# Last norm of a mixture-of-experts stage split into three steps, GpSimd's order written out, and two experts that finish their tokens in place

## The chip, the cores and the metric

The kernel runs on one core of a Trainium2 chip (trn2). The metric is the device time of one execution in microseconds (us), lower is better; three runs of the kernel before gave 2713.91, 2713.98 and 2725.86 us, median 2713.98 us.

## The reference, cut to what matters

2048 tokens of width 1024, all in float32, pass a first block, a second mixer with its norm, cross attention with its norm, and last a grouped mixture of experts (MoE) with a residual and a layer norm. Only that last part is touched.

```python
def grouped_moe(x, router_w, router_bias, w_gate, w_up, w_down):
    scores = sigmoid(xt @ router_w)                       # 16 experts in 4 groups of 4
    sel = scores + router_bias
    best = argmax(sum of the top 2 of sel in each group)  # one group for each token
    _, idx = top_k(where(in_grp, sel, -inf), 2)           # two experts, both of that group
    gate = scores[idx] / sum(scores[idx])
    # for each expert, blocks of 128 of its tokens:
    hb = silu(xb @ w_gate[e]) * (xb @ w_up[e])            # 1024 -> 256
    yb = hb @ w_down[e]                                   # 256 -> 1024
    return sum over the two experts of gate * yb

x = layer_norm(DEEPNORM_ALPHA * x + grouped_moe(x, ...), ln_moe_g, ln_moe_b)
```

## The kernel before, in words

Matrix products are done in float32 by splitting each operand in a rounded high part (a cast on ScalarE, line 173) and a low part (a subtraction on VectorE or GpSimd, line 174), and three matmuls (`mm3`). Weights come by DMA from SyncE's queue (`rawload`), six loads of 512 KB for an expert, into a ring of seven buffers, and are split as they come.

The MoE stage, `moe()`, starts at about 2222 us of the span and lasts to its end. By then a DRAM table `x3d` holds each token's row and its gates, and a DRAM table `sumd` holds the scaled residual, to which the experts' results are added. The router has put, for each expert, the numbers of its tokens into a table `tabi`. `BLOCKS` says how many blocks of 128 tokens an expert has a place for: two or three. The first two are one **unit** (`n` = 2, matmuls over 256 tokens), a third is a unit of its own (`n` = 1) that uses the same weights: 23 units in all, in the order of the experts 0 to 15. Tokens beyond that would be worked off in a loop at the end (`For_i` over `nit`); for these inputs it runs no pass.

`run` emits the units as a pipeline. In the iteration of a unit `u` (its neighbours are `v`, the next, and `w`, the one after):

1. `u.up(0)`: half of gate and up, 48 matmuls (24 for a third block); splits of down weights; `u.act(0)`: tanh on ScalarE, two steps on VectorE (lines 1175, 1176), a cast and a subtraction.
2. `turn` of the unit before (two transposes, third blocks alone), then the hook `mids`.
3. `u.up(1)`, `u.act(1)`; the transposes of `v`'s gathered tokens (line 240) with their splits; the last gate-and-up weights of `v`; the indirect gather of `w`'s tokens on GpSimd's queue (line 1126).
4. `down` of the unit before: 12 matmuls for a block, scaled on ScalarE out of PSUM (line 1200), and an indirect scatter-add into `sumd` on GpSimd's queue (line 1201). Each scatter-add waits until those of the unit before and the fetches since have landed, since rows may be the same.
5. The hook `late`, then the splits of `w`'s weights.

The last norm needs a token's finished sum. A token's two experts are of one group, so a group's tokens are done when its four experts are. For them a second table `tabgi` lists the tokens of each group in blocks of 128 (`NFIN` blocks: 4, 5, 5, 4, and 2 for the tokens of expert 15, which comes last). `last_norm`, called by the hooks as `FETCH` says (one or two blocks for an expert from expert 5 on), fetches one block of sums (`fetch`, line 1395) and at the same place finishes the block fetched one expert earlier (`finish`): statistics on VectorE (line 1410), one over the standard deviation by two small GpSimd instructions (lines 192 and 194, result `fr`), two passes over 128x1024 on VectorE (line 1417 with the mean, line 1418 with `fr`), and an indirect write to the output on GpSimd's queue (line 1419). At the end stand the blocks of the last groups, first with statistics alternating between VectorE and ScalarE (lines 1405, 1406).

What sets the order: ScalarE and VectorE run in the order in which the program is written (`MANUAL`). The orders of TensorE and GpSimd come from the tile scheduler, which places each instruction where its own estimate of time puts it. Each engine runs its list in order, so an instruction that waits holds all behind it on its engine; GpSimd is also the engine that issues all indirect DMAs.

## Time and profile before

| | us |
|---|---|
| median of three runs | 2713.98 |
| the profiled execution: its time | 2722.46 |
| the profiled execution: span, first to last instruction | 2720.7 |
| of the span: up to the MoE stage | 2222 |
| MoE stage: 2222 to the last matmul | 458 |
| after the last matmul, to the end of the span | 40 |

An execution's time is 1.8 us more than its span (2722.46 less 2720.7). The profiled execution is 8.5 us longer than the median of the three runs. TensorE is busy for 94% of the whole span; in the MoE stage the granted clock, the waits of TensorE and the stretch after the last matmul are what is to be read, and the section of rows below has them. The profile's chain of waits reaches back only 1.3 us from the end here and says nothing.

### The profile page before, as it was taken

To read this page: it belongs to the slowest core of one execution; us is meant where nothing else is said; L and a number is where in the kernel's file an instruction comes from. 1 tells how busy PE (TensorE), PEld (TensorE's weight loads), DVE (VectorE), ACT (ScalarE), POOL (GpSimd) and SP (SyncE) were. 2 spreads that over 40 slices of the span, in tenths; PEclk is the share of its full clock that TensorE was granted. 3 is DMA by queue.
4 is the path that set the end of the run, shared out by engine and by line. 5 is a ranking of instruction groups with operands and counts; after the bars stand their busy time and mean duration, and the time that the engine had idled before them with its cause. 6 is when DMAs were issued, how large, how long until landed. Compare 5 with 4: busy or idle time off the path is not lost. (4 is left out here: it accounts for less than half of the span.)

```text
span 2720.7 us, 36998 instructions
## 1 busy us (share of the span) xinstructions
PE 2549.0 (94%) x13954; PEld 2156.0 (79%) x13954; DVE 1608.8 (59%) x3228; ACT 1136.1 (42%) x2023; POOL 597.4 (22%) x635
## 2 busy tenths in 40 slices
PE   8899999999999999999999999999999969989882
PEld 8777788777878887778788878778888859978872
DVE  5536366766454666665456666563667457666554
ACT  5644353242444532434354333343532325444442
POOL 0102202211021031101201221021032133445445
PEclk9999999999999999999999999999999979999986
DMA  8861351444224325441242345312415357878755
GB/s 299 287 217 55 109 163 55 154 152 145 92 77 133 117 64 169 155 141 48 84 161 72 116 144 197 94 55 87 162 47 183 104 180 264 247 237 254 223 153 138
DMA packets 121557, 396.81 MB, mean 146 GB/s; under 512 B 15264, under 2 KB 15408, under 8 KB 121376
## 3 DMA queue, kind: packets, MB, share of 16 engines
q1 hardware_dynamic: 104144, 334.01, 36.6%
q0 software_dynamic: 17232, 60.42, 8.4%
q8 instruction: 110, 1.80, 0.3%
q14 instruction: 71, 0.58, 0.1%
HBM read 314.87 MB, written 81.60 MB: 146 GB/s over the span
## 5 line engine op out<-in xcount | busy, mean ns | idle before, releaser
L183 PE MATMUL bank<-rounded 128*128 128x512 f32 (+2 forms) x10628 | 2198.8, 364 | 73.4 <-ACT rounded L173 54.1
L183 PEld LDWEIGHTS bank<-rounded 128*128 128x128 f32 x10628 | 1773.3, 192 | 380.4 <-ACT rounded L173 61.5
L174 DVE TENSOR_TENSOR rounded<-work,rounded 128x1024 fp32r<-128x1024 f32 (+3 forms) x531 | 577.7, 1100 | 476.4 <-ACT rounded L173 430.4
L173 ACT CAST rounded<-work 128x1024 fp32r<-128x1024 f32 (+3 forms) x564 | 512.5, 926 | 691.2 <-PE bank L183 251.8
L173 ACT CAST rounded<-bank 128x512 fp32r<-128x512 f32 (+1 forms) x220 | 112.0, 555 | 219.1 <-PE bank L240 98.1
L183 PE MATMUL bank<-work 128*128 128x128 f32 (+5 forms) x944 | 163.6, 301 | 6.9 <-DVE work L525 2.2
L183 PEld LDWEIGHTS bank<-work 128*128 128x128 f32 (+1 forms) x944 | 130.7, 190 | 37.0 <-issue 5.1
L174 DVE TENSOR_TENSOR rounded<-bank,rounded 128x512 fp32r<-128x512 f32 (+1 forms) x220 | 133.0, 639 | 42.5 <-ACT rounded L173 40.6
L240 PE MATMUL bank<-ident,work 128*128 128x128 f32 x712 | 98.2, 283 | 28.4 <-ACT work L345 8.6
L240 PEld LDWEIGHTS bank<-ident,work 128*128 128x128 f32 x712 | 82.2, 145 | 46.3 <-ACT work L345 13.4
L192 POOL TENSOR_SCALAR lnrv<-lnmv 128x1 f32<-128x1 f32 x32 | 40.6, 1269 | 283.3 <-DVE lnmv L672 283.1
L375 POOL TENSOR_SCALAR work<-work 128x512 f32<-128x512 f32 x32 | 25.4, 793 | 345.9 <-ACT work L374 345.9
L665 DVE SCALAR_TENSOR_TENSOR work<-work,bank 128x512 f32<-128x512 f32 x64 | 43.8, 685 | 73.3 <-PE bank L183 73.1
L1201 POOL DMA_INDIRECT sumd<-work,tabi x39 | 72.1, 1849 | 35.1 <-ACT work L1200 15.7
L174 POOL TENSOR_TENSOR rounded<-work,rounded 128x1024 fp32r<-128x1024 f32 (+1 forms) x33 | 65.9, 1997 | 38.1 <-ACT rounded L173 35.4
L754 DVE SCALAR_TENSOR_TENSOR work<-work,c_convT 128x512 f32<-128x512 f32 x96 | 71.9, 749 | 2.5 <-ACT work L752 0.7
L1126 POOL DMA_INDIRECT work<-x3d,tabi x39 | 47.9, 1228 | 113.9 <-issue 42.1
L859 POOL TENSOR_TENSOR work<-work 128x512 f32<-128x512 f32 (+6 forms) x40 | 46.2, 1154 | 112.3 <-ACT work L851 110.4
L192 POOL TENSOR_SCALAR rrmsv<-ssq 128x1 f32<-128x1 f32 x34 | 11.2, 329 | 261.4 <-DVE ssq L570 172.7
L795 POOL TENSOR_TENSOR work<-work,ar 128x520 f32<-128x520 f32 x16 | 17.0, 1062 | 232.8 <-DVE work L757 177.3
L906 POOL TENSOR_SCALAR work<-work,xrv 128x256 f32<-128x256 f32 x64 | 30.1, 484 | 152.3 <-DVE xrv L904 152.3
L1200 ACT ACTIVATE work<-bank,gr 128x512 f32<-128x512 f32 x78 | 51.1, 702 | 29.4 <-PE bank L183 13.0
(320 smaller groups left out, 2148.1 us busy)
## 6 DMA issues: line engine op xcount, KB each, us to landing
work<-in_w_gu SPq DMA_DIRECT2D x64, 512.0 KB
work<-in_x SPq DMA_DIRECT2D x32, 512.0 KB
work<-in_w_out SPq DMA_DIRECT2D x32, 512.0 KB
work<-wmp SPq DMA_DIRECT2D x32, 512.0 KB
work<-wxa SPq DMA_DIRECT2D x32, 512.0 KB
work<-wvw SPq DMA_DIRECT2D x32, 512.0 KB
work<-in_w_dn SPq DMA_DIRECT2D x32, 512.0 KB
sumd<-work SPq DMA_DIRECT2D x19, 512.0 KB
```

The costliest lines, as they stand in the source:

```text
L173: ACT.copy(hi, src)
L174: (lo_eng or DVE).tensor_sub(lo, src, f32(hi))
L183: PE.matmul(o, l, r, start=start, stop=stop)
L192: POOL.tensor_scalar(v, src, scale, eps, op0=OP.mult, op1=OP.add)
L240: PE.transpose(p[:, k * 128:(k + 1) * 128], src[:, (4 * hf + k) * 128:(4 * hf + k + 1) * 128], ident)
L665: DVE.scalar_tensor_tensor(oh_, xr, ALPHA, a, op0=OP.mult, op1=OP.add)
L754: DVE.scalar_tensor_tensor(s, z[:, k:k + T], conv[:, k, c:c + 1], s, op0=OP.mult, op1=OP.add)
L859: POOL.tensor_tensor(nx[:, lo:], cur[:, lo:], cur[:, lo - d_:15 + T - d_], op=OP.add)
L906: POOL.tensor_scalar(P[:, h, :], P[:, h, :], rv[:, h:h + 1], 0.0, op0=OP.mult, op1=OP.add)
L1126: POOL.indirect_dma_start(out=xg, out_offset=None, in_=x3d[:, :], in_offset=at)
L1200: ACT.activation(y[:, hs], a, AF.Copy, scale=self.gc[r])
L1201: d = POOL.indirect_dma_start(out=sumd[:, :], out_offset=self.at[r], in_=y, in_offset=None, compute_op=OP.add)
```

## The change

- **Order of the experts.** `ORDER` is 0 to 7, 12, 13, 8, 9, 10, 14, 11, 15.
- **Finished in place.** Experts 11 and 15 (`FINAL`) stand at the end of their groups, 2 and 3. Each of their blocks fetches the sums of its tokens ahead (`sums`), VectorE adds the gated result out of PSUM to them (line 1228 in the changed kernel, in the place of ScalarE's scaling), and the block is normed and written from there. The sum is still written to `sumd`, now by a plain scatter in the place of the adding one. Their tokens leave the group tables: `NFIN` is 3, 5, 2, 3, so 13 blocks are fetched for the norm in the place of 20, and 5 more are finished in place.
- **Three steps.** `fetched` (the new hook `turn`, before the gather of `w` and before `down`) fetches one or two blocks; `measure`, in the next iteration's `mids`, takes the statistics and `fr`; `norms`, in that iteration's `late`, does the two passes and the write. The loose constants of `FETCH` are gone: one block is fetched, or two where three or more are ready or a `FINAL` unit comes next.
- **GpSimd's order.** `queued` ties each GpSimd instruction of the stage that it is given to the one before, without a wait, so that the scheduler keeps the written order. The small scalar step (line 193) is left free.
- **Buffers.** The key and value tables of the first block are joined as `sks`, whose first 1024 columns serve as a fourth buffer `FX` of fetched sums.
- **The end.** The last three blocks of group 3 have statistics and the multiplication by `fr` on ScalarE and the addition of the bias on GpSimd (line 1461, `shared`); the blocks of experts 11 and 15 have theirs on VectorE, with statistics on ScalarE for every first one.

```diff
+ORDER = 0, 1, 2, 3, 4, 5, 6, 7, 12, 13, 8, 9, 10, 14, 11, 15
+FINAL = 11, 15
-FETCH = {5: (1, 0), 6: (1, 0), 7: (1, 0), ...}
...
-    NL = 5
-    NFIN = 4, 5, 5, 4, 2
+    NL = 4
+    NFIN = 3, 5, 2, 3
...
+        FX = rotate([FX((128, D)) for _ in range(3)] + [sks[:, 0:D]])
...
+        def queued(*ds_):
+            if line[0]:
+                for d in ds_:
+                    for o in line[1]:
+                        tc.add_manual_dep(d.ins, o.ins.name, mybir.DependencyInfo(
+                            mybir.DependencyClass.NoSync, mybir.DependencyReason.DATA), reason="order")
+            line[1] = ds_
+            return ds_[0]
...
+            def sums(self, mem):
+                self.z = [fetch(at, mem)[0] for at in self.at]
...
-                    y = YT((128, D))
+                    y = self.z[r] if self.final else YT((128, D))
...
-                        ACT.activation(y[:, hs], a, AF.Copy, scale=self.gc[r])
+                        if self.final:
+                            DVE.scalar_tensor_tensor(y[:, hs], a, self.gc[r], y[:, hs], op0=OP.mult, op1=OP.add)
+                        else:
+                            ACT.activation(y[:, hs], a, AF.Copy, scale=self.gc[r])
                     d = POOL.indirect_dma_start(out=sumd[:, :], out_offset=self.at[r], in_=y, in_offset=None,
-                                                compute_op=OP.add)
+                                                compute_op=OP.bypass if self.final else OP.add)
...
+                    if self.final:
+                        queued(d)
+                        measured.append((y, self.at[r], *stats(y, DVE if r else ACT), True, YT))
...
                     v.weights_up([3])
+                    if i in turn:
+                        turn[i]()
                     if w:
                         w.gather()
                     if i:
                         units[i - 1].down()
                     if i in late:
                         late[i]()
...
+        def scaled(z, at, mean, op, r, static=True, mem=None, shared=False):
+            x = mem((128, D)) if mem else z
+            DVE.scalar_tensor_tensor(x, z, mean, gains[:, 0], op0=op, op1=OP.mult)
+            if shared:
+                ACT.activation(x, x, AF.Copy, scale=r)
+                queued(POOL.tensor_tensor(x, x, gains[:, 1], op=OP.add))
+            else:
+                DVE.scalar_tensor_tensor(x, x, r, gains[:, 1], op0=OP.mult, op1=OP.add)
+            d = POOL.indirect_dma_start(out=out[:, :], out_offset=at, in_=x, in_offset=None,
...
+        def fetched(j):
+            if units[j].final:
+                units[j].sums(FX)
+            if j == N - 2:
+                fetches(len(ready), XG)
+            elif not units[j].final:
+                fetches(1 if len(ready) < 3 and not units[j + 1].final else 2)
+
+        for j in range(5, N - 1):
+            mids[j], turn[j], late[j] = measure, lambda j=j: fetched(j), norms
...
         def last():
-            last_norm(30, 1)
-            group_done(3)
-            last_norm(0, NFIN[3], XG)
+            norms()
+            measure(ACT, 1)
+            units[N - 1].sums(MRAW)
+
+        mids[N - 1], late[N - 1] = last, lambda: (measure(ACT), norms())
```

On **GpSimd**, where a block is fetched in the middle of the stage (before: around expert 11; in the rows `x3d` is a gather of tokens, `sumd<-work` a scatter-add, `work<-sumd` a fetch for the norm, `frv` and `fr` the two small instructions, `out_dram` the write), there stands before:

```order
L1126 DMA work<-x3d,tabi 128x1040
L1201 DMA sumd<-work,tabi 2432x1024
L1395 DMA work<-sumd,tab 128x1024
L192 TENSOR_SCALAR frv_17216<-fmv_17208 128x1
L194 TENSOR_TENSOR fr_17220<-frv_17216,mhalf 128x1
L1419 DMA out_dram<-work,tab 2048x1024
L1126 DMA work<-x3d,tabi 128x1040
```

and now, where the third block of expert 12 and the first two of expert 13 are worked on, up to the gathers for expert 8:

```order
L1436 DMA sks<-sumd,tab 128x1024
L1436 DMA work<-sumd,tab 128x1024
L1146 DMA work<-x3d,tabi 128x1040
L1231 DMA sumd<-work,tabi 2432x1024 x2
L193 TENSOR_SCALAR frv_17049<-fmv_17041 128x1
L195 TENSOR_TENSOR fr_17053<-frv_17049,mhalf 128x1
L193 TENSOR_SCALAR frv_17050<-fmv_17042 128x1
L195 TENSOR_TENSOR fr_17054<-frv_17050,mhalf 128x1
L1436 DMA work<-sumd,tab 128x1024 x2
L1146 DMA work<-x3d,tabi 128x1040 x2
L1231 DMA sumd<-work,tabi 2432x1024
```

Before, the fetch of a block stands between the scatter-adds and the `fr` of another block, and one gather of each pair stands ahead of the adds. Now the fetches stand ahead of the gathers and the adds, and `fr` stands ahead of the next fetches; both gathers of a pair stand behind the fetches.

On **VectorE**, in the iteration of a unit of two blocks (before: expert 11; `bank` is PSUM, `L1175` and `L1176` are `act`, `fmv` the statistics), there stands before:

```order
L174 TENSOR_TENSOR rounded<-bank_70,rounded 128x128
L1410 BN_STATS fst_17211<-work 128x6 x2
L1411 BN_AGGR fmv_17208<-fst_17211 128x2
L1417 SCALAR_TENSOR_TENSOR work<-work,fmv_17208 128x1024
L1418 SCALAR_TENSOR_TENSOR work<-work,fr_17220 128x1024
L1175 SCALAR_TENSOR_TENSOR work<-work,bank_71 128x256
L1176 TENSOR_TENSOR work<-work,bank_71 128x256
```

and now (expert 13):

```order
L1451 BN_STATS fst_17045<-sks 128x6 x2
L1452 BN_AGGR fmv_17041<-fst_17045 128x2
L1451 BN_STATS fst_17044<-work 128x6 x2
L1452 BN_AGGR fmv_17042<-fst_17044 128x2
L1198 SCALAR_TENSOR_TENSOR work<-work,bank_67 128x256
L1199 TENSOR_TENSOR work<-work,bank_67 128x256
L175 TENSOR_TENSOR rounded<-work,rounded 128x256
L175 TENSOR_TENSOR rounded<-bank_68,rounded 128x512
L175 TENSOR_TENSOR rounded<-bank_69,rounded 128x512
L1339 COPY gr_15872<-work 128x1
L1458 SCALAR_TENSOR_TENSOR sks<-sks,fmv_17041,work 128x1024
L1463 SCALAR_TENSOR_TENSOR sks<-sks,fr_17053,work 128x1024
```

Only the statistics are left ahead of the second activation (`L1198`, before `L1175`); the pass that needs `fr` has moved behind it and behind the splits of the next unit's tokens.

On **GpSimd**, at the very end, there stands now, from the fetch of expert 15's sums on (`out_dram<-work,tab` are group 3's blocks, `out_dram<-work,tabi` those of expert 15):

```order
L1436 DMA work<-sumd,tabi 128x1024 x2
L193 TENSOR_SCALAR frv_17049<-fmv_17041 128x1
L195 TENSOR_TENSOR fr_17053<-frv_17049,mhalf 128x1
L1461 TENSOR_TENSOR work<-work 128x1024
L1464 DMA out_dram<-work,tab 2048x1024
...
L1464 DMA out_dram<-work,tab 2048x1024
L1231 DMA sumd<-work,tabi 2432x1024
L195 TENSOR_TENSOR fr_17054<-frv_17050,mhalf 128x1
L1231 DMA sumd<-work,tabi 2432x1024
L195 TENSOR_TENSOR fr_17055<-frv_17051,mhalf 128x1
L1464 DMA out_dram<-work,tabi 2048x1024 x2
```

Before, the last matmuls were followed by two scatter-adds, two fetches that wait for them, and the norms of both; now the two scatters stand between the norms, and no fetch is left behind the last matmul.

## Rows read from the trace of the kernel before

**Rows 1.** Head of the page.

```profile
span 2720.7 us, 36998 instructions
```

**Rows 2.** Windows: stretch, length, busy by engine (instructions), PEclk, DMA share, GB/s.

```profile
2240.00:2360.00 120.00, 119.01 (x885) 113.71 (x883) 85.82 (x193) 65.36 (x101) 44.47 (x27) 0.99 0.80 249
2360.00:2660.00 300.00, 261.43 (x1743) 240.93 (x1742) 184.90 (x308) 133.21 (x229) 138.12 (x108) 0.93 0.74 218
2680.00:2721.00 41.00, 0.31 (x2) 0.00 (x0) 17.62 (x18) 7.88 (x14) 22.57 (x23) 0.53 0.42 124
```

**Rows 3.** Waits, 2390 to 2660: who <- for whom: us in total, times, longest.

```profile
POOL work L1395 <- DMA sumd<-work,tabi: 40.8, 7, 9.2
DVE work L1418 <- POOL fr L194: 40.4, 11, 6.9
...
PE bank L183 <- ACT rounded L173: 28.3, 7, 7.2
```

**Rows 4.** TensorE's waits alone, 2390 to 2660.

```profile
PE bank L183 <- POOL rounded L174: 5.9, 2, 3.9
```

**Rows 5.** Timeline, 2511 to 2528: start, us, engine, line [idle before <- releaser].

```profile
2511.54 1.58 POOL L1201 DMA_INDIRECT sumd<-work,tabi  x1 [0.30 <-issue]
...
2522.44 1.00 POOL L1395 DMA_INDIRECT work<-sumd,tab  x1 [9.32 <-issue]
...
2523.78 0.57 POOL L194 TENSOR_TENSOR fr<-frv,mhalf 128x1 f32<-128x1 f32 x1
2524.39 1.28 DVE L1418 SCALAR_TENSOR_TENSOR work<-work,fr 128x1024 f32<-128x1024 f32 x1 [6.06 <-POOL fr L194]
...
2527.43 8.39 PE L183 MATMUL bank<-rounded 128*128 128x256 f32 x48 [4.91 <-ACT rounded L173]
```

**Rows 6.** TensorE's timeline, pieces after waits and pieces without.

```profile
2488.88 8.81 PE L183 MATMUL bank<-rounded 128*128 128x256 f32 x48 [3.99 <-ACT rounded L173]
...
2567.20 1.91 PE L240 MATMUL bank<-ident,work 128*128 128x128 f32 x16
...
2580.31 6.00 PE L183 MATMUL bank<-rounded 128*128 128x256 f32 x48
...
2586.93 3.01 PE L183 MATMUL bank<-rounded 128*128 128x512 f32 x12
...
2628.19 7.59 PE L183 MATMUL bank<-rounded 128*128 128x256 f32 x48 [4.32 <-ACT rounded L173]
...
2642.37 13.43 PE L183 MATMUL bank<-rounded 128*128 128x512 f32 x68 [3.91 <-POOL rounded L174]
...
2675.20 5.11 PE L183 MATMUL bank<-rounded 128*128 128x512 f32 x12 [7.71 <-ACT rounded L173]
```

**Rows 7.** DMA issues, 2230 to 2660: count, median us from issue to landing.

```profile
work<-x3d,tabi POOLq DMA_INDIRECT x39, 8.3
sumd<-work,tabi POOLq DMA_INDIRECT x36, 8.9
work<-sumd,tab POOLq DMA_INDIRECT x13, 4.2
```

**Rows 8.** Instructions that write or read `sumd`, 2340 to 2610: DMA landing.

```profile
DMA to landing us min/median/max: 4.2/8.9/12.0
```

**Rows 9.** GpSimd's groups, 2230 to 2721: count, busy us, mean ns.

```profile
L1201 POOL DMA_INDIRECT sumd<-work,tabi x39 | 72.1, 1849 | 35.1 <-ACT work L1200 15.7 <-issue 9.9 <-DMA work<-sumd,tab 4.5
...
L174 POOL TENSOR_TENSOR rounded<-work,rounded 128x1024 fp32r<-128x1024 f32 x13 | 35.0, 2691 | 2.4 <-ACT rounded L173 2.3
L1419 POOL DMA_INDIRECT out_dram<-work,tab x20 | 22.6, 1129 | 20.3 <-DVE work L1418 14.8 <-DVEq L1471 1.6 <-DMA work<-sumd,tab 1.6
```

**Rows 10.** Timeline after the last matmuls: a pair of ScalarE statistics, and the last instruction.

```profile
2672.38 1.06 ACT L1405 ACTIVATE junk<-work 128x1024 bf16<-128x1024 f32 x1 [7.20 <-DMA work<-sumd,tab]
...
2674.67 0.19 ACT L1406 ACTIVATION_READ_ACCUMULATOR junk<-work,fmv 128x1 f32 x1
...
2711.73 1.03 POOL L1419 DMA_INDIRECT out_dram<-work,tab  x1 [1.61 <-DVEq L1471]
```

107 lines of the change are left out of this document (62 added, 45 removed).

## The prediction, as it was put on record

> **What bounds the kernel now.** I first read the windows by stage. From 2240 to 2360, with no norm yet, TensorE is busy 119.0 of 120 us at full granted clock; from 2360 to 2660, where norms run beside the experts, it is busy 261.4 of 300 at a mean clock of 0.93; from 2680 to the end at 2720.7 it does nothing [rows 1, 2]. So TensorE bounds the stage, and it loses time in two ways: it waits among the norms, and nothing is left for it at the end.
>
> Then the waits, to see for whom it waits. Between 2390 and 2660 it waits seven times, 28.3 us, for a cast of ScalarE (line 173), and twice, 5.9 us, for a weight split on GpSimd [rows 3, 4]. VectorE waits 40.4 us in 11 pieces for `fr`, and GpSimd's fetches wait 40.8 us for scatter-adds to land [rows 3].
>
> Last the timeline, where these are one chain. GpSimd issues a scatter-add at 2511.54; the fetch behind it can only be issued at 2522.44, 10.9 us later; `fr` of another block, which needs neither, stands behind it and is made at 2523.78; VectorE's second pass starts at 2524.39 after 6.06 us of waiting, and only then come the activation steps behind it; TensorE starts again at 2527.43 after 4.91 us [rows 5]. VectorE's pass ends at 2525.67, so the activation and the casts take 1.8 us more. That a norm is late costs nothing by itself; that the activation stands behind it in VectorE's list does.
>
> **The waits that go.** The change takes the pass with `fr` out from in front of the activation, and `fr` out from behind a blocked fetch. The seven waits (28.3) and the two for GpSimd's late split (5.9) are 34.2 us [rows 3, 4]. What hides the passes now is the matmuls of `down` and of the next unit's first half. I take all 34.2 as gone; the bound below is that those for GpSimd stay (28.3), since its list is as full as before.
>
> After such a wait the matmuls are slow, too: 48 of them take 6.00 us where none precedes, and 8.81, 8.39 and 7.59 after waits of 3.99, 4.91 and 4.32 [rows 5, 6], that is 2.8, 2.4 and 1.6 us more, 2.3 on average. This is the granted clock falling from 2.4 GHz to 1.2 for a while. Of the nine waits, six are over 2.9 us; six times 2.3 is 13.8 us. Bounds: nothing, and the 21 us that 0.93 of 300 us leaves, idle time included [rows 2].
>
> **The waits that come.** GpSimd's list is now fixed, and its fetches and scatter-adds wait for one another: a fetch for the landing of the last add, an add for the landing of the fetches. Both gathers of a unit stand behind the fetches. The worst place is where two iterations in a row fetch two blocks each, before expert 8's gathers. From the issue of the add of expert 7's third block: first fetch at 10.9 (as in [rows 5]), second at 12.2 (1.00 and a gap of 0.30), landed 4.2 later at 16.4 [rows 7]; two adds for expert 12, the second 1.85 + 0.30 later at 18.6 [rows 9]; its landing, again 10.9, lets the next fetch go at 29.5, the second at 30.8, the gathers at 32.1 and 33.4; they land 8.3 later, at 40.4 and 41.7 [rows 7]. Beside that TensorE has: the third block of expert 12 with 6.00, transposes for expert 13 with 1.91, expert 12's down with two times 3.01; expert 13's 12.0, its third block's transposes of half 1.91, the down of a third block 3.0, the next 48 matmuls 6.00 [rows 6]: 35.9 us together. The second tile's transposes can wait the 0.95 of the first, so the wait is 41.7 - 0.95 - 35.9 = 4.9 us; with 2.3 for slow matmuls 7.2. The same chain stands once more, from the add of expert 10's third block over experts 14 and 11 to the gathers for expert 15. Two times 7.2 is 14.4 us. Adds landing at their median of 8.9 rather than 10.9 would take 4 us from each chain and leave 0.9; at the largest, 12.0 [rows 8], it is 2.2 more, 7.1.
>
> In front of experts 5 and 6 the statistics of two blocks now stand where VectorE has the group tables to work out; I put 2 us there, between 0 and the 3 us or so that GpSimd's and VectorE's small steps of two blocks take.
>
> Everything else has one answer. The 20 blocks become 18, off the path. The order of experts moves no work of TensorE. The joined table `sks` leaves the first block's instructions in their order. Finishing in place trades ScalarE's scaling for a VectorE addition out of PSUM of the same size. GpSimd gets one more power step for nothing.
>
> **The end.** Before, the first half of expert 15's matmuls ends at 2642.37 + 13.43 = 2655.8 [rows 6] and the span at 2720.7 [rows 1]: 64.9 us, with 7.71 of waiting before the last matmuls [rows 6], two adds that must land, two fetches, and their norms. Counted from the same point, the new end has, in ScalarE's list, the second half (6.0) and expert 11's third block (3.0), 9.0; three pairs of statistics of 2.5 (2672.38 to 2674.86 [rows 10]), 16.5; the activation 1.8 and as an estimate 0.4 for the tanh ahead of it, 18.7; a fourth pair 21.2; a scaling of 1.1 as the 1.06 pass in [rows 10], 22.3. From there GpSimd is the bound: three additions of 128x1024, which I price as its 2.69 us subtraction of the same shape, each with a write of 1.13 and a gap of 0.30 [rows 9]: 12.4, to 34.7; then two scatters of 1.85 + 0.30 and two powers of 0.57 [rows 5, 9], 5.4, to 40.1; VectorE's last pass 1.28 [rows 5] and a gap, 41.7; from the issue of the last write to the end of the span 9.0 (2711.73 to 2720.7 [rows 1, 10]): 50.7. Ahead of it stand four fetches that wait for the add of expert 14's third block and hold back expert 11's norms, which in VectorE's list stand in front of expert 15's first activation: 10.9, three times 1.3, a landing of 4.2, a scatter of 2.15, a power of 0.57 and three passes of 1.28 are 25.6 us from the issue of that add, beside TensorE's 6.0 + 1.91 + 6.02 + 6.0 = 19.9 up to the point counted from. So expert 11's third block can start 25.6 - 19.9 + 2.2 = 7.9 us after it, where 6.0 was counted, and up to 7.9 later where other small steps come between; or on time, if TensorE's own 4.9 us for expert 15's gathers cover it. I take the middle of 0 and 7.9, 4.0, and get 54.7. The end becomes 64.9 - 54.7 = 10.2 us shorter; bounds 14.2 and 6.3.
>
> The Trainium skill, page "SBUF — State Buffer", section "Who interferes with whom", says that a VectorE instruction with two SBUF inputs and a GpSimd instruction that reads SBUF exclude each other for a whole instruction. The three additions run beside norm passes of that kind; if each waited out one pass, the end would be 3.9 us longer (an estimate from 1.28 a pass), and the forecast as much later. No row of before has these additions, so nothing here bears it out yet.
>
> **The sum.** 34.2 + 13.8 + 10.2 = 58.2 saved, 14.4 + 2 = 16.4 lost: 41.8 us. The profiled execution of 2722.46 would take 2681; it is 8.5 above the median, and so the median of 2713.98 becomes about 2672.
>
> **The rivals.**
> 1. *The gathers come in time.* If adds land sooner in the smoother order, both new waits vanish: 16.4 less 2 more, 14.4 saved, 2658. For it: the DMA share is no higher than 0.80 in either stretch [rows 2], and the median landing is 2 us below what I took [rows 7]. Against: the same bytes in less time. The Trainium skill, page "DMA: Bandwidth & Descriptors", section "Anatomy of one DMA — SWDGE (gpsimd) path", gives 2.0 us and the bytes over 436 GB/s for one transfer, an estimate of 3.2 us for 512 KB; by that this rival is what happens. The trace has 8.9 for the adds [rows 7] and disagrees.
> 2. *GpSimd's list becomes the bound in more places.* With adds landing at 12.0, each of the two chains costs 7.1 + 2.3 = 9.4, and two more, at experts 5 to 6 and in the last units, cost as much: 37.6 instead of 16.4. With nothing gained at the end, 58.2 - 10.2 - 37.6 = 10.4 saved, 2704; half of it gives 2688. For it: the largest landing is 12.0 [rows 8]. Against: it is the largest, not the median.
> 3. *Slower: every gather behind a fetch comes late.* Eight iterations fetch blocks. A wait w in each costs 8 (w + 2.3), against 34.2 + 13.8 = 48.0 that the old waits give back. It decides from w = 3.7 on; at 7.7, 80 - 48 = 32 us are lost, 2746. For it: before, one gather of each pair stood ahead of adds and fetch, and now none does. Against: with one turn of add and fetch the chain is 10.9 + 1.3 + 1.3 + 8.3 = 21.8 us, and TensorE has at least 12.0 + 0.95 + 3.0 + 6.0 = 22 beside it; only two places have two turns.
> 4. *It does not do what it says.* If VectorE met `fr` late all the same, because GpSimd's power step waits behind adds, the waits stay and the end alone gains its 10.2: 2704. Against: the listed orders have the power step ahead of the next fetches. The tables could also overflow into the loop at the end; but the reference's routing gives the four lists 380, 546, 243 and 382 tokens, which 3, 5, 2 and 3 blocks hold.
>
> **How the numbers follow.** Forecast 2672 (own range 2662 to 2688) 0.55; rival 1 0.20; rival 2, from 2688 to 2704, 0.14; rival 4 0.06; rival 3 0.05. Leaving out half of rival 1 below and rivals 3, 4 and part of 2 above, the range is 2655 to 2698. A change within 0.5%, 13.6 us, is about what a measurement here can't tell from none: faster than 2700.4 is the forecast, rival 1 and most of rival 2, 0.88; within, 0.07; slower, rival 3, 0.05.
>
> **What would show it.** Right: between 2360 and the last unit TensorE's long waits on line 174/173 splits are gone, VectorE waits for `fr` only at the end, the two longest waits left are for gathers of expert 8 and expert 15, and the stretch behind the last matmul is about 20 us where it was 40. Wrong: TensorE waiting for gathers in most iterations with a fetch, scatter-adds landing in under 8 us or over 12, or GpSimd not being the last to finish.

## The result, and the profile after

The changed kernel takes 2690.03 us in the median of four runs (2686.61 to 2690.54) where the kernel before takes 2718.27 (2713.91 to 2725.86): a ratio of 0.9886, with a 95% interval of 0.9864 to 0.9909. That is faster by the 0.5% of the prediction, inside its range of 2655 to 2698, and 18 us above its 2672. The profiled execution takes 2690.54 us, its span 2688.8, against 2720.7 before [rows 1]: 31.9 us less where 41.8 were forecast.

For the accounts below the MoE stage is cut at two places that both kernels have: TensorE's first wait of note, ahead of the 12 matmuls of expert 4's third block (2360.96 before, 2361.38 after), and the transposes of expert 11's third block, 0.2 us before the end of expert 15's first half (2655.64 before, 2631.63 after). Ahead of the first place 0.4 us are lost, between the two 24.4 are won (294.7 to 270.3), behind the second 7.9 (65.1 to 57.2).

The windows view, core 0, gives busy time by engine, then the granted clock, the DMA share and GB/s. First the changed kernel:

```profile
2240.00:2360.00 120.00, 119.01 (x879) 113.82 (x879) 83.78 (x191) 63.65 (x99) 44.76 (x28) 0.98 0.79 244
2361.40:2631.80 270.40, 248.74 (x1717) 233.03 (x1717) 175.98 (x298) 132.66 (x222) 129.40 (x103) 0.95 0.80 241
2660.00:2689.00 29.00, 1.15 (x4) 0.58 (x2) 9.26 (x12) 3.98 (x6) 19.07 (x16) 0.56 0.36 137
```

The stretch of the kernel before that answers to the second row:

```profile
2361.00:2655.80 294.80, 257.06 (x1717) 237.24 (x1717) 182.70 (x302) 131.18 (x222) 137.53 (x108) 0.93 0.74 218
```

The same 1717 matmuls stand in both stretches, so the 24.4 us split exactly: TensorE's idle time falls from 37.7 (294.80 - 257.06) to 21.7 (270.40 - 248.74), 16.1 us, and its busy time by 8.3, which on balance is matmuls that no longer run slowly after a wait.

Who TensorE waits for in that stretch of the changed kernel (us in total, times, longest; the rows of before are [rows 3, 4]):

```profile
PE bank L243 <- DMA work<-x3d,tabi: 15.9, 4, 8.4
PE bank L184 <- ACT rounded L174: 3.9, 2, 3.1
PE bank L184 <- POOL rounded L175: 2.5, 2, 2.0
```

The waits for ScalarE's casts, 28.3 us in seven pieces before, are one of 3.09 and one of 0.81. In their place stand waits for gathers, 15.9 us. TensorE's timeline shows where (start, duration, instruction, idle time before and what ended it):

```profile
2367.53 0.80 PE L184 MATMUL bank<-rounded 128*128 128x256 f32 x2 [3.09 <-ACT rounded L174]
...
2473.05 3.67 PE L243 MATMUL bank<-ident,work 128*128 128x128 f32 x16 [3.27 <-DMA work<-x3d,tabi]
...
2496.69 1.06 PE L243 MATMUL bank<-ident,work 128*128 128x128 f32 x8 [1.18 <-DMA work<-x3d,tabi]
2497.51 3.23 PE L184 MATMUL bank<-rounded 128*128 128x512 f32 x14
2509.17 0.87 PE L243 MATMUL bank<-ident,work 128*128 128x128 f32 x3 [8.43 <-DMA work<-x3d,tabi]
2509.69 13.33 PE L184 MATMUL bank<-rounded 128*128 128x256 f32 x94
2522.86 1.58 PE L243 MATMUL bank<-ident,work 128*128 128x128 f32 x13
...
2613.24 3.40 PE L243 MATMUL bank<-ident,work 128*128 128x128 f32 x16 [3.04 <-DMA work<-x3d,tabi]
...
2640.55 7.12 PE L184 MATMUL bank<-rounded 128*128 128x512 f32 x24 [2.78 <-ACT rounded L174]
2656.03 5.12 PE L184 MATMUL bank<-rounded 128*128 128x512 f32 x12 [8.37 <-ACT rounded L174]
```

The reader is to see four late gathers, of experts 8 (3.27), 9 (1.18), 10 (8.43) and 15 (3.04), and two waits at the end. The one for expert 10 is the longest of the stage, and nothing in the prediction speaks of it. It is odd, too: three of its 16 transposes wait, and behind them stand 94 matmuls, nearly all of both halves of expert 9, which need nothing of expert 10.

GpSimd's timeline at the end shows what is last:

```profile
2656.32 1.02 POOL L1436 DMA_INDIRECT work<-sumd,tabi  x1 [0.19 <-issue]
...
2660.70 2.35 POOL L1461 TENSOR_TENSOR work<-work 128x1024 f32<-128x1024 f32 x1
...
2668.76 2.37 POOL L1461 TENSOR_TENSOR work<-work 128x1024 f32<-128x1024 f32 x1
...
2675.01 2.02 POOL L1231 DMA_INDIRECT sumd<-work,tabi  x1 [0.19 <-issue]
2677.07 0.70 POOL L195 TENSOR_TENSOR fr<-frv,mhalf 128x1 f32<-128x1 f32 x1
2677.96 2.02 POOL L1464 DMA_INDIRECT out_dram<-work,tabi  x1 [0.19 <-issue]
2680.28 0.97 POOL L1464 DMA_INDIRECT out_dram<-work,tabi  x1 [0.31 <-issue]
```

GpSimd has hardly a gap from 2656 to the last write. The last matmul ends at 2661.2, 27.7 us before the end of the span; before it was 40.4.

### The profile page after: what moved, and what is told of

It is laid out like the page before. It is cut to its first block, busy times and chain, and to the rows that moved or that the text cites. A ratio compares the mean times of both kernels' runs of the same rounds, so it can differ in the third digit from the quotient of the medians.

```text
span 2688.8 us, 36967 instructions
## 1 busy us (share of the span) xinstructions
PE 2543.1 (95%) x13954; PEld 2155.1 (80%) x13954; DVE 1597.7 (59%) x3218; ACT 1139.1 (42%) x2024; POOL 588.0 (22%) x630
## 5 line engine op out<-in xcount | busy, mean ns | idle before, releaser
L184 PE MATMUL bank<-work 128*128 128x64 f32 (+4 forms) x944 | 163.6, 301 | 7.0 <-DVE work L529 2.1
L243 PEld LDWEIGHTS bank<-ident,work 128*128 128x128 f32 x712 | 84.4, 148 | 62.6 <-DMA work<-x3d,tabi 14.6
L1231 POOL DMA_INDIRECT sumd<-work,tabi x38 | 63.1, 1661 | 151.0 <-ACT work L1230 105.2
L1197 ACT ACTIVATE work<-bank 128x256 f32<-128x256 f32 (+1 forms) x46 | 16.2, 352 | 102.8 <-PE bank L184 99.1
L184 PE MATMUL bank<-sks,work 128*128 128x64 f32 (+2 forms) x384 | 57.4, 319 | 2.5 <-ACT work L473 1.4
```

What stands on the lines that cost most here:

```text
L184: PE.matmul(o, l, r, start=start, stop=stop)
L243: PE.transpose(p[:, k * 128:(k + 1) * 128], src[:, (4 * hf + k) * 128:(4 * hf + k + 1) * 128], ident)
L1231: d = POOL.indirect_dma_start(out=sumd[:, :], out_offset=self.at[r], in_=y, in_offset=None, compute_op=OP.bypass if self.final else OP.add)
```

## The experiments

Twelve kernels were run, each beside the kernel before on the same chip. "Stage" and "end" are the two stretches defined above, in the profiled execution. The kernels "changed", endold, actlast and dve have the same stage, and it took 265.6 to 270.3 us in them: under 5 us, one profile's stage says little.

| kernel | ratio to the kernel before, 95% interval | stage, us | end, us |
|---|---|---|---|
| before | 1 | 294.7 | 65.1 |
| changed | 0.9886 (0.9864 to 0.9909) | 270.3 | 57.2 |
| twostep | 0.9864 (0.9847 to 0.9880) | 263.9 | 60.2 |
| noq | 0.9899 (0.9877 to 0.9920) | 275.8 | 53.6 |
| swap | 0.9902 (0.9876 to 0.9928) | 277.8 | 56.7 |
| deep | 0.9850 (0.9834 to 0.9866) | 257.2 | 57.5 |
| thinw | 0.9817 (0.9801 to 0.9833) | 255.3 | 57.3 |
| free | 0.9848 (0.9829 to 0.9867) | 264.4 | 52.7 |
| order | 0.9839 (0.9819 to 0.9858) | 256.8 | 57.6 |
| endold | 0.9947 (0.9930 to 0.9964) | 267.4 | 75.6 |
| actlast | 0.9909 (0.9889 to 0.9930) | 265.6 | 63.1 |
| dve | 0.9863 (0.9844 to 0.9883) | 265.6 | 54.1 |
| best1 | 0.9829 (0.9813 to 0.9845) | 253.8 | 48.0 |
| best2 | 0.9837 (0.9820 to 0.9853) | its transposes stand elsewhere | |

### Which part took the old waits away

**twostep** puts the passes back in front of the activation:

```diff
-            mids[j], turn[j], late[j] = measure, lambda j=j: fetched(j), norms
+            mids[j], turn[j], late[j] = lambda: (measure(), norms()), lambda j=j: fetched(j), norms
```

> The changed kernel with one part undone: the two passes of a norm stand right behind its statistics, ahead of the second half's activation, as before the change; GpSimd's fixed list, the order of experts and the finishing in place stay. Theory P (place of the pass): the waits of 28.3 us for casts of ScalarE came from VectorE standing with the pass in front of the activation; most of them and of their slow matmuls return: 2710 to 2725. Theory F (fr behind a blocked fetch): it was GpSimd's list that made fr late; with fr now ahead of the fetches the pass costs TensorE next to nothing: 2690 to 2696.

The intervals of the two ratios overlap, and theory P's time did not come. But the place of the pass is not free. TensorE's timeline in twostep:

```profile
2374.31 0.80 PE L184 MATMUL bank<-rounded 128*128 128x256 f32 x2 [8.27 <-ACT rounded L174]
...
2520.68 1.91 PE L243 MATMUL bank<-ident,work 128*128 128x128 f32 x16
```

In the stage TensorE waits 14.6 us for ScalarE in four pieces, 10.7 more than in the changed kernel: 2.76 and 2.75 in the place of the seven old waits, and 8.27 at experts 5 and 6, where the changed kernel has 3.09. The time does not show it, since TensorE waits only 2.8 us for gathers, where the changed kernel has 15.9: in twostep all 16 transposes of expert 10 stand behind expert 9's matmuls (the second row), and none of them waits; "order" below comes back to this.

**noq** takes the fixed list away and keeps the three steps:

```diff
-            line[0] = True
+            line[0] = False
```

> The changed kernel (2690 us where the kernel before takes 2718) without GpSimd's fixed list: what it does, and in which order, is left to the scheduler as before; the three steps, the order of experts and the finishing in place stay. The run with the passes put back in front of the activation gave no loss, so the place of the pass was not what cost 34 us. Theory F (the fixed list did it, since fr no longer stands behind a blocked fetch): fr comes late again; 2700 to 2715, with ScalarE casts waited for again. Theory E (either one is enough: with the passes behind the activation a late fr holds up nothing that TensorE wants): 2686 to 2695, VectorE waiting longer for fr and TensorE not.

```profile
PE bank L184 <- POOL rounded L175: 23.7, 2, 13.4
...
PE bank L184 <- ACT rounded L174: 2.3, 2, 2.1
...
```

The rows are TensorE's waits from 2361 to 2640 in noq. Theory E holds: the time is that of the changed kernel, and ScalarE is hardly waited for, though `fr` is late again: VectorE waits 21.5 us for it in this stage (15.7 and 5.8), and not at all in that of the changed kernel. So with the pass behind the activation a late `fr` does no harm; and with `fr` in time a pass in front of the activation brings back only 5.5 of the 28.3 us of [rows 3] (twostep), though it lengthens the wait at experts 5 and 6. No run undoes both at once: that the old waits then return is argued from the chain of [rows 5], not shown. The order of experts did not take them away, for with the old order they are gone, too ("order" below: 4.0 us of waiting for ScalarE); finishing expert 11 in place was not tried apart. What the list does change is which wait comes instead: without it two weight splits on GpSimd are late (10.34 and 13.35), with it four gathers.

### Why the gathers are late

Two theories stood at first. A (list): GpSimd issues a gather late, behind fetches and adds that wait for one another. B (bytes): it is issued in time and lands late, because the DMA engines are full.

**swap** puts the gathers ahead of the fetches of the same iteration.

```diff
+                    if w:
+                        w.gather()
                     if i in turn:
                         turn[i]()
-                    if w:
-                        w.gather()
```

> The changed kernel (2690.0 us) with the gathers of the next unit but one ahead of the iteration's fetches in GpSimd's list; all else as it is. In the changed kernel TensorE waits 3.27, 1.18, 8.43 and 3.04 us for the gathers of experts 8, 9, 10 and 15. Theory A (list): a gather is late because GpSimd issues it late. Then the waits of experts 8 and 15, behind two fetches each (2.6 to 3.0 us of issue), fall to about 0.4, that of expert 9, behind one fetch (1.8), to 0; expert 10's iteration fetches nothing, so its 8.43 stay: 7 us less waiting and about 3 of slow matmuls, 2680. Theory B (bytes): a gather is late because the DMA engines are full; from 2480 to 2520 their share is 0.96 and 0.99. Then each gather lands when it did, and the time is 2687 to 2691.

```profile
2481.46 4.77 PE L184 MATMUL bank<-rounded 128*128 128x512 f32 x14 [5.01 <-POOL rounded L175]
2516.27 0.87 PE L243 MATMUL bank<-ident,work 128*128 128x128 f32 x3 [13.21 <-DMA work<-x3d,tabi]
2628.63 11.78 PE L184 MATMUL bank<-rounded 128*128 128x512 f32 x61 [6.46 <-POOL rounded L175]
```

These are TensorE's long waits in swap. Those for experts 8, 9 and 15 are gone, as A has it, and the time is no better: the fetches are later, so the adds that wait for their landing are, and behind the adds the weight splits (5.01 and 6.46) and expert 10's gathers (13.21). Scaled to the 2718.27 of before, its ratio gives 2691.6 us: B's time within 1 us, but not for B's reason, since three of the four gathers did come in time.

**thinw** loads a quarter of each weight row from expert 8 on, so that the DMA engines have less to move and every list is as it was. The expectation's "11 MB" was too small; between 2340 and 2600 they move 49.18 MB where the changed kernel has 66.24.

```diff
-        SP.dma_start(raw, src)
+        if thin[0]:
+            SP.dma_start(raw[:, 0:256], src[:, 0:256])
+        else:
+            SP.dma_start(raw, src)
...
+            units[-1].thin = e > 7
```

> The changed kernel with a quarter of each weight row loaded from expert 8 on (256 of 1024 columns; the rest of the tile keeps old values, so the product is another one), every instruction, queue and order as before: the DMA engines have some 11 MB less to move. Theory A (list): GpSimd issues expert 10's gathers as late as before, and at least 5 of its 8.43 us of waiting stay; 2684 to 2690. Theory B (bytes): its gathers land in 6 us where they took 11 to 12, the wait of 8.43 falls under 2, and those of experts 8, 9 and 15 vanish: 2668 to 2674. Between them: issued 4.5 us late and 3.9 us slow gives about 4.5 us of waiting at expert 10.

The first of GpSimd's gathers for expert 10 in the changed kernel (TensorE's wait for them, at 2509.17, is shown above):

```profile
2496.95 1.04 POOL L1146 DMA_INDIRECT work<-x3d,tabi  x1 [0.19 <-issue]
```

The same gather in thinw, and TensorE's wait for them:

```profile
2491.34 1.05 POOL L1151 DMA_INDIRECT work<-x3d,tabi  x1 [0.19 <-PE bank L188]
...
2496.29 0.52 PE L247 MATMUL bank<-ident,work 128*128 128x128 f32 x3 [0.43 <-DMA work<-x3d,tabi]
```

In the changed kernel TensorE wants them 3.8 us after their issue (2509.17 - 8.43 - 2496.95) and has them after 12.2; in thinw it wants them 4.5 us after the issue and has them after 5.0. The list is about as late in both; the landing is 7 us sooner. So at this place B holds: full DMA engines turn a short lead into 8.43 us. Some of the whole gain will be other loads that land sooner.

**deep** issues the gathers one unit earlier.

```diff
-            for j in range(min(2, n)):
+            for j in range(min(3, n)):
...
-                    if w:
-                        w.gather()
+                    if i + 3 < n:
+                        units[i + 3].gather()
```

> The changed kernel with the gathers of a unit issued one unit earlier (three units ahead, where the four gather buffers were half empty), at the same place in the iteration. Theory A (list): every gather lands some 15 to 25 us before it is wanted, the 15.9 us of waiting for gathers are gone and with them 4 to 6 us of slow matmuls: 2669. Theory B (bytes): the same bytes have to pass between 2480 and 2520, and then the weights come late instead of the gathers; at most half is saved: 2680 or more, with TensorE waiting for splits of weights of experts 9 and 10.

```profile
2482.43 4.86 PE L184 MATMUL bank<-rounded 128*128 128x512 f32 x14 [5.61 <-POOL rounded L175]
2611.41 12.21 PE L184 MATMUL bank<-rounded 128*128 128x512 f32 x68 [4.80 <-POOL rounded L175]
```

No wait for a gather is left, and the kernel is faster, by less than A's forecast and with an interval that just touches that of the changed kernel: the two weight splits on GpSimd now come late (the rows). Also, with six gathers ahead of the first expert the stage itself begins later: from GpSimd's write of `x3d` to the first cut it takes 143.3 to 143.6 us in deep and in the two kernels that build on it, 140.1 in the changed kernel, and 136.9 to 138.5 in the ten others.

**free** removes the other wait: adds no longer wait for the landing of list blocks, whose rows belong to tokens that the experts to come do not hold.

```diff
...
                     for o in adds + reads:
                         after(d, o)
+                    for o in apart_reads:
+                        apart(d, o)
...
-        def fetch(at, mem):
+        def fetch(at, mem, own=True):
...
-            reads.append(queued(d))
+            queued(d)
+            if own:
+                reads.append(d)
+            else:
+                apart_reads.append(d)
...
-                got.append(fetch(ready.pop(0), mem))
+                got.append(fetch(ready.pop(0), mem, False))
```

> The changed kernel (2690 us where the kernel before takes 2718) with one kind of wait taken away: a scatter-add of an expert no longer waits for the landing of the list blocks' fetches, which read rows of tokens that the experts still to come do not hold. Fetches still wait for the adds before them, and those of expert 11's and 15's own sums keep both waits. Theory A (list: the turns of fetch and add hold GpSimd back, 21.2 us in 4 pieces): expert 8's and 15's gathers and the split at expert 11 come 3 to 6 us earlier, TensorE waits 8 to 10 us less, 2678 to 2682. Theory B (bytes: what is issued lands when the DMA engines have room): expert 10's 8.43 us stay or grow, since more is under way at once; 2685 to 2691.

```profile
2472.63 1.09 PE L243 MATMUL bank<-ident,work 128*128 128x128 f32 x8 [1.17 <-DMA work<-x3d,tabi]
2474.32 1.09 PE L243 MATMUL bank<-ident,work 128*128 128x128 f32 x8 [0.59 <-DMA work<-x3d,tabi]
...
2505.82 0.87 PE L243 MATMUL bank<-ident,work 128*128 128x128 f32 x3 [6.87 <-DMA work<-x3d,tabi]
...
2609.14 1.09 PE L243 MATMUL bank<-ident,work 128*128 128x128 f32 x8 [0.74 <-DMA work<-x3d,tabi]
```

The median of 2678.55 (against 2718.43) is what A gave, though the ratio's interval still touches that of the changed kernel. Experts 8 and 15 wait 1.76 and 0.74 us in the place of 3.27 and 3.04. The four kernels with the same stage show what chance does there: they wait 2.43 to 3.59 at expert 8 and 0.96 to 4.74 at expert 15. So about half of expert 8's wait was A's, and for expert 15 that is likely and not shown. Expert 10 still waits 6.87, so most of its 8.43 (8.04 to 8.46 in the four) was not.

**order** puts experts 12 and 13 back behind 10.

```diff
-ORDER = 0, 1, 2, 3, 4, 5, 6, 7, 12, 13, 8, 9, 10, 14, 11, 15
+ORDER = 0, 1, 2, 3, 4, 5, 6, 7, 8, 9, 10, 12, 13, 14, 11, 15
```

> The changed kernel with experts 12 and 13 behind expert 10 again; only 11 stays moved, ahead of 15. Between the lists' blocks the five of list 1 are then fetched beside experts 8 and 9 of two blocks each, whose iterations are short, and no longer beside 12 and 13 of three. Theory A (list): the gathers for experts 9 and 10, behind two fetches each and in short iterations, come 5 to 10 us later: 2695 to 2700. Theory B (bytes): it is the run of short experts 8, 9, 10, in which weights, gathers, adds, fetches and writes meet, that costs; it stands in both orders, so the time stays within 4 us, 2686 to 2694, with the longest wait still at expert 10's gathers.

```profile
PE bank L243 <- DMA work<-x3d,tabi: 7.7, 4, 3.5
...
```

Neither theory had this: 2678.98, a ratio wholly below that of the changed kernel, with the long wait gone (the rows, TensorE's waits from 2361 to 2626). So the changed kernel with its order of experts 12 and 13, which the prediction costed at nothing, loses 0.5% against the old order. The listed instructions of TensorE show what differs. In the changed kernel they stand, around expert 9, as

```
1505 L184 MATMUL bank_66<-rounded 128x512 x6
1506 L184 MATMUL bank_67<-rounded 128x512 x6
1507 L184 MATMUL bank_68<-rounded 128x256
1508 L184 MATMUL bank_69<-rounded 128x256
1509 L243 MATMUL bank_70<-ident,work 128x128 x3
1510 L184 MATMUL bank_68<-rounded 128x256 x47
1511 L184 MATMUL bank_69<-rounded 128x256 x47
1512 L243 MATMUL bank_70<-ident,work 128x128
```

Rows 1507, 1508, 1510 and 1511 are expert 9's two halves; row 1509 is three transposes of expert 10, ahead of 94 of those 96 matmuls. TensorE's list is left to the scheduler, which put them there in the changed kernel. The order of experts does not settle it alone: twostep has the same order and has them behind. Such 94 matmuls take 11.54 us where no wait precedes (the kernel before, at 2365.28), so in their usual place the transposes would be wanted at 2500.74 + 11.5 = 2512.3, and the gathers are there at 2509.2: by these times the whole 8.43 us hang on that place. The kernels bear it out. Changed, swap, free, endold, actlast and dve have the three transposes ahead of expert 9's halves, and TensorE waits 8.43, 13.21, 6.87, 8.29, 8.46 and 8.04 us there; thinw has them, too, and waits 0.43, since its gathers land in 5 us; twostep and order have all 16 in one piece, and no wait at that place (order's longest, 3.46 and 2.49 us, are for expert 14's two tiles). (noq, deep and best1 spread them among expert 9's matmuls in several pieces, with 1.78 us at most.) No run moved the three transposes alone, so a part of order's gain may lie elsewhere, in where the list blocks' fetches fall; and where twostep, noq, deep or best1 are compared with the changed kernel, this place is in the difference.

### What sets the end

Theory S: ScalarE's list, with its statistics ahead of expert 15's second activation, or the round trip through `sumd`. Theory G: GpSimd's list.

**endold** lets expert 15 add to `sumd`, fetch and norm as before; expert 11 stays.

```diff
-                        POOL if e < POOL_FIRST else DVE, 3 < e < 15, of, e in FINAL)
+                        POOL if e < POOL_FIRST else DVE, 3 < e < 15, of, e == 11)
...
-            units[N - 1].sums(MRAW)
...
+        finish([fetch(at, MRAW) for at in units[N - 1].at], (DVE, ACT))
```

> The changed kernel with expert 15 as before: its products are scaled, added to the sums in DRAM, and fetched and normed when the adds have landed; expert 11 still finishes in place. Theory S (the round trip is what the end saves): an add's landing of 8 to 11 us, two fetches of 1.3 and a landing of 4 to 5.5 come into the end, two dead scatters of 1 to 2 us go: 10 to 13 us slower, 2700 to 2703. Theory G (GpSimd's list of three additions and their writes, which runs to 2673 anyway, sets the end): the round trip is half hidden beside it, 3 to 6 us slower, 2693 to 2696.

```profile
2674.96 1.58 POOL L1231 DMA_INDIRECT sumd<-work,tabi  x1 [0.30 <-issue]
2682.81 1.01 POOL L1436 DMA_INDIRECT work<-sumd,tabi  x1 [6.26 <-issue]
2684.13 0.96 POOL L1436 DMA_INDIRECT work<-sumd,tabi  x1 [0.30 <-issue]
2688.93 1.28 POOL L193 TENSOR_SCALAR frv<-fmv 128x1 f32<-128x1 f32 x1 [3.84 <-DVE fmv L1452]
```

It costs more than either theory had: 2705.06, the end 18.4 us longer. The adds can only be issued behind the three additions, and from the second add's issue to the first fetch it is 7.9 us, then 4.8 to the step that follows the first statistics. Finishing expert 15 in place is worth more than the 7.9 us by which the whole end became shorter (18.4 in these two profiles), so the rest of the new end gives some back.

**actlast** puts the last blocks' statistics behind expert 15's second activation.

```diff
             norms()
-            measure(ACT, 1)
             units[N - 1].sums(MRAW)
```

> The changed kernel with ScalarE's statistics of the last list blocks behind expert 15's second activation instead of ahead of it. In the changed kernel TensorE waits 8.37 us there before its last 12 matmuls. Theory S (ScalarE's list sets the end): the wait is gone, the last matmuls end 8 us earlier, and so does the span: 2682. Theory G (GpSimd's list sets the end): the three additions can start no earlier than now, the statistics behind the activation come some 2 us later, and the end stays within 2 us: 2688 to 2692.

Theory S falls, and the time is G's: the ratio is not better. But the end is 63.1, 5.9 us longer, where G allowed 2. The last matmuls still wait 6.92 us, now for a cast and an activation behind the norm of expert 11's third block, and the statistics that were moved make the additions start later.

**dve** has the last list blocks' second passes on VectorE.

```diff
-                measured.append((x, at, *stats(x, on), True, None, on is ACT))
+                measured.append((x, at, *stats(x, on), True, None, False))
```

> The changed kernel with the second pass of the last three list blocks on VectorE (1.28 us each) instead of a scaling on ScalarE and an addition on GpSimd (2.35, 2.35 and 2.37 us). Theory G (GpSimd's list sets the end): 7.1 us of it go, VectorE has 7.0 us idle there; last write 5 to 7 us earlier: 2683 to 2685. Theory S (ScalarE's list and the last matmuls behind it set the end): within 2 us, 2688 to 2692.

2681.97 against 2717.92, a gain in the direction of G, with the end 3.1 us shorter and the intervals of the ratios overlapping; the stage, which the edit does not touch, is 4.7 us shorter in this profile, too, so not all of the gain is the end's. From the last matmul to the end it is 22.8 us where the changed kernel has 27.7. The last matmuls still wait 8.35 us.

### Together

**best1** joins free, deep and dve. **best2** adds another order at the end: expert 11's third block goes first, expert 15's second activation comes ahead of the norms left.

> Three edits together: adds that no longer wait for list fetches, gathers one unit earlier, and the second pass of the last list blocks on VectorE. Gathers one unit earlier alone took out the 15.9 us of waiting for gathers and brought 10.4 us of waiting for GpSimd's weight splits, which stood behind adds that waited for fetches. If that reading is right, these splits now come in time (under 2 us of waiting in all), the stage is some 20 us shorter and the end 3 to 5: 2664 to 2670. If the DMA engines' load is what sets the stage, the splits' waits turn into others (casts of weights that land late): 2674 to 2682.

> The kernel with those three edits and another order at the end: expert 11's third block is turned and multiplied down ahead of expert 15's first half, expert 15's second activation stands ahead of all norms left, and expert 11's norms behind both activations. Theory N (expert 11's norms in VectorE's list, ahead of expert 15's first activation, and behind it the round trip of its third block's scatter and expert 15's fetch, set the end): the 2.8 and 8.4 us of waiting before the last matmuls go, the last write comes 8 to 10 us earlier: 2655 to 2660. Theory G (GpSimd's scatters, fetches and writes at the end set it): 2 to 4 us, 2661 to 2667.

best1 takes 2669.51 us against 2718.43: it beats both kernels, and its interval lies below that of the changed one. Two splits are still late, 3.66 and 4.79 us, which its expectation had not. best2 takes 2674.4, so theory N falls as a way to go faster: the two waits before the last matmuls are gone, the last matmul comes 27.4 us after the wait for expert 11's split (37.5 in best1), and the stretch behind it, 37.1 us for 22.5, loses it again. One piece of that is a pass of VectorE that waits for a buffer whose block is still being written:

```profile
2644.00 1.28 DVE L1469 SCALAR_TENSOR_TENSOR work<-work,fmv 128x1024 f32<-128x1024 f32 x1 [2.98 <-DMA out_dram<-work,tabi]
```

best1 with the order of experts of "order" would be the next kernel to try; it was not run.

## Why the prediction was right, and where it was off

**The waits that go: right but for 2.5 us, the reason half right.** 34.2 us of long waits were to go. ScalarE's 28.3 went; of the 5.9 for GpSimd's weight splits 2.5 stay, 2.02 of them at expert 11, which had 3.91 before. 3.5 of short ones were to stay, and 21.7 - 15.9 = 5.8 are left that are not for gathers; 3.09 of that is the step at experts 5 and 6, counted below. The text named two causes in a row, `fr` behind a blocked fetch and the pass ahead of the activation. noq shows that to move the pass is enough, and twostep that `fr` in time does most of it, so the change pays twice for most of one gain.

**The slow matmuls: right.** 13.8 back and 4.6 lost, 9.2 net; the busy time of the 1717 matmuls fell by 8.3. The granted clock of the stage rose from 0.93 to 0.95.

**The waits that come: too small by 6.4 us.** Forecast 11.8 of waiting (twice 4.9, and 2), with the 3.5 that were to stay 15.3; measured 21.7. The chains at experts 8 and 15 were found at the right places, and priced 4.9 where 3.27 and 3.04 came; that adds and fetches which wait for one another make them is borne out by free for half of expert 8's wait, and not clear of chance for expert 15. The landings of the adds from 2340 to 2600 were 8.0 in the median, not 10.9. The step in front of experts 5 and 6 was 3.09 for 2.

The step that failed is the one sentence "The order of experts moves no work of TensorE", and with it the silent premise that TensorE's list stays as it was: no term stands for it. The amount of work is the same, but in the changed kernel's list three transposes of expert 10 stand in front of 94 matmuls of expert 9. That wait is 8.43 us, and the 94 matmuls behind it take 13.33 in the place of 11.54, 1.8 more: 10.2 us. The listed instructions of TensorE show it; the prediction drew on those of GpSimd and VectorE alone. The trace of the kernel before has such a place already, without a wait: eight transposes of expert 7, two and six, ahead of 94 matmuls of expert 6.

```profile
2364.68 0.82 PE L240 MATMUL bank<-ident,work 128*128 128x128 f32 x6
2365.28 11.54 PE L183 MATMUL bank<-rounded 128*128 128x256 f32 x94
```

That 10.2 us is about the whole miss of 9.9 is chance. Ahead of the stage 0.4 us are missing, at the end 2.3, in the stage 7.2, and there the 10.2 stand against experts 8 and 15, whose waits were priced 3.5 us too high. And of the 18 us by which the median lies above the forecast, these 9.9 are the sum's; the other 8 come from carrying over that the profiled execution of before was 8.5 us above its median, where that of the changed kernel is 0.5 above.

**The end: 57.0 for 54.7**, counted from the prediction's own point (2619.59 + 12.20 = 2631.79). The third block of expert 11 began 2.8 us late (the 2.78 of TensorE's wait). The prediction took 4.0, the middle of 0 and 7.9; but by its own working the block could start 7.9 us after that point where 6.0 was counted, which is 1.9 late, so the 4.0 follows from no row; the measured 2.8 lies between. The first of ScalarE's statistics started 14.3 us after that point, for 13.0, since VectorE's addition out of PSUM stands between; and behind the first pair comes a weight cast that the sum had left out (ScalarE's timeline):

```profile
2646.05 1.06 ACT L1446 ACTIVATE junk<-work 128x1024 bf16<-128x1024 f32 x1 [5.22 <-issue]
...
2648.44 1.03 ACT L174 CAST rounded<-work 128x1024 fp32r<-128x1024 f32 x1
2649.37 1.05 ACT L1446 ACTIVATE junk<-work 128x1024 bf16<-128x1024 f32 x1
```

GpSimd's additions took 2.35 to 2.37 us for 2.69. endold shows that the round trip which they replaced is worth more than the end as a whole gained.

**The rivals.** The 2690 lies outside the forecast's own 2662 to 2688 and inside the whole range. Rival 1 (gathers in time) did not come, though in thinw, with three quarters of the late weights gone, it nearly does (0.83 us at most). The Trainium skill, page "DMA: Bandwidth & Descriptors", section "Anatomy of one DMA — SWDGE (gpsimd) path", would have 3.2 us for 512 KB by its figures, an estimate; the trace disagrees again, with 8.0 for adds and 8.1 for gathers, and 5.9 for gathers in thinw. Rival 2's mechanism (GpSimd's list the bound in more places) is part of the truth: 2690 lies in its range, yet the largest single piece was TensorE's list and not GpSimd's. Rivals 3 and 4 did not happen: four gathers were late by up to 8.43 us, in one iteration beyond the 7.7 of rival 3, but most came in time.

**What would show it.** VectorE does wait for `fr` only at the end, 12.4 us in four pieces (40.4 in 11 before). The two longest waits were not the gathers of experts 8 and 15, and the stretch behind the last matmul is 27.7 us, not 20. Of the signs of being wrong none came, though the adds' landing, 8.0, is at the edge of one.

## What to carry to other kernels

When a change reorders units of work and one engine's list is left to a scheduler, read that engine's list, the bound's first of all: a few instructions of the next unit hoisted over a long run of ready ones turn a late load into a stall of the whole engine. The same list can hide what an edit costs: twostep brought back 10.7 us of waits and was no slower, since its list lacked that stall. Two cures for the same stall need not add up; before both are paid for, try each alone, and once neither. And to take away one engine's waits (here by gathering earlier) shows the next instruction in the same list that was late all along (here weight splits behind adds), so that cures for a list have to be made together.

## What the runs showed of the hardware

VectorE was held up by GpSimd where both read two operands from SBUF. A VectorE subtraction of a weight split takes 1.22 us alone, and 2.40 beside GpSimd's. GpSimd's and VectorE's timelines of the changed kernel:

```profile
2617.11 2.42 POOL L175 TENSOR_TENSOR rounded<-work,rounded 128x1024 fp32r<-128x1024 f32 x1
2618.24 2.40 DVE L175 TENSOR_TENSOR rounded<-work,rounded 128x1024 fp32r<-128x1024 f32 x1
2638.05 1.22 DVE L175 TENSOR_TENSOR rounded<-work,rounded 128x1024 fp32r<-128x1024 f32 x1
```

Another VectorE pass beside GpSimd's addition took 3.76 us where the same pass takes 1.28. The same two engines in actlast:

```profile
2658.51 2.35 POOL L1461 TENSOR_TENSOR work<-work 128x1024 f32<-128x1024 f32 x1
2658.19 3.76 DVE L1458 SCALAR_TENSOR_TENSOR work<-work,fmv 128x1024 f32<-128x1024 f32 x1
```

The Trainium skill, page "SBUF — State Buffer", section "Who interferes with whom", which the prediction weighed, says that such instructions exclude each other; these rows agree that one waits for the other. That it is for a whole instruction they do not show: in actlast VectorE's pass began 0.32 us before the addition and was still the one held up. In these two pairs the price was paid by VectorE; GpSimd's additions kept their 2.35 to 2.38 us. In the changed kernel's end no pass stood beside one long enough to matter (1.33 at most), so the 3.9 us that the prediction set aside (three times 1.28 are 3.8) did not come.

TensorE had expert 10's first gather 12.2 us after its issue where the DMA share was 0.96 to 0.99 (2480 to 2520), and 5.0 us after it with three quarters of the weights left out, where the share was 0.85 (2480 to 2500 in thinw). These are one gather each.
